# A TensorE stream that keeps the order of the program

## The chip, the cores and the metric

The kernel runs on one core of a Trainium2 chip. A core has five engines that work side by side, each on its own list of instructions and in the order of that list: TensorE (PE, matrix products), VectorE (DVE), ScalarE (ACT), GpSimd (POOL) and SyncE (SP, which here issues DMA transfers). An instruction that needs a result of another engine, or a buffer that another engine still reads, waits at the head of its list on a semaphore. The metric is the device time of one execution in microseconds (us).

## The reference

One inference step of a two-layer streaming encoder on 1024 prompt tokens and 32 sample tokens (1056 in all), width 1024, in float32. Cut to what matters:

```python
for l in range(2):
    sh1, sc1, g1, sh2, sc2, g2 = split(silu(c) @ w_ada[l] + b_ada[l], 6)     # adaLN columns
    u = x * (1 + sc1) + sh1
    if l == 0:      # mLSTM: q, k, v, gates, o from u @ w_in; a short convolution and silu on q and k
        y = mlstm_mixer(u, ...)          # 4 heads; state C (256 x 128), n, m carried from chunk to chunk
    else:           # shared k, v = (x * (1 + kv_scale) + kv_shift) @ w_kv
        q = u @ w_q
        y = softmax(q k^T / 8 + bias over own chunk and 8 previous ones) v @ w_out
    x = layer_norm(ALPHA * x + (1 + g1) * y)
    u = x * (1 + sc2) + sh2
    f = square(relu(u @ w_up[l])) @ w_down[l]
    x = layer_norm(ALPHA * x + (1 + g2) * f)
```

Inside a head the mLSTM needs per chunk the scores of the chunk, the values `num`, a new state, and a norm of the head's output. Outputs are `x`, the states, and the newest keys and values.

## The kernel before

**Products.** Tokens stand along the free dimension, features on the partitions, in three blocks of 384, 384 and 288 tokens (`TBS`). A float32 product is three passes over two float32r parts of each operand (`proj`, L111 to L120), so a 128-column tile of a product over 1024 features is 24 matmuls. Weights come by DMA as raw float32 and are split into their two parts by ACT and by DVE or POOL (`split`, L87 to L90).

**Stages, in order.**
- Start: the first adaLN columns come from TensorE (`ada`, L392); the tokens are transposed on TensorE (`xps`, L375) and modulated by ACT and DVE into U; `v_proj` (L440 to L475) makes the values and gate inputs of head 0, tile by tile (`v_0_0` to `v_0_8`, L455 to L457).
- Gates: `gate_rows` (from L477) transposes the gate inputs (`gt`, L492), runs the recurrences of the gates on DVE and ACT up to `stk` (L520), yields, and then transposes the result back on TensorE (`ae_ps`, L527).
- mLSTM: for each head, `qk_proj` and `v_proj` of the next head are advanced tile by tile, and after each tile the generator `mlstm` (L587 to L690) of the current head does one step: `scores` of chunk i (L616, L617), `values` of chunk i-1 (`num` L634 to L636, the state's `cu` L638, then a chain of small DVE and ACT operations up to `hn`, L664), and `heads` of chunk i-2 (`hT`, L672). `num` and `cu` share two PSUM banks (`nmt`). At the same time the adaLN columns of the rest of layer 0 are multiplied on DVE (`ada_l0`, through `ada_cols`, L223 to L253: products L236, transpose L243, sum `cx` L244) and every eight columns go once through TensorE (`adas`, L250).
- `o_proj` for the output gates, in two halves; then `flow.finish()`, which drains all side work; then the output projection (`op_a`), layer norm (means and variances by TensorE, `mean_n` and `var_n`, L843) and the MLP of layer 0 (`up`, `dn`).
- Layer 1: query projection (`q`), cached keys and new keys and values (`put_keys`, transposes `kt_c` L1138; `kv` products), banded attention (scores `s` L1225, softmax on DVE, ACT and POOL, transposes `pt` L1255, values `pv` L1275), output projection, MLP, and the last layer norm.

**What sets the order.** Side work is written as generators. A `Flow` (L47 to L72) holds them; `flow.tick(us)` after each tile of main work subtracts us from each generator's wait and advances those whose wait is over, and `flow.finish()` runs them out. So the program text has one order, in which main tiles and side steps alternate. Before, this order isn't the order on the engines: a list scheduler of the framework goes over the whole program with its own estimates of durations and puts each engine's instructions in the order in which it expects them to be ready. It works on each engine; the PSUM banks and SBUF buffers follow from it.

Of the kernel before, what the change touches and what calls it, by code (L numbers as in the profile page):

```python
# [8 lines left out]
F32 = mybir.dt.float32  # L9
# [6 lines left out]
P = 128  # L16
D = 1024
KC = D // P                     # feature chunks
TP = 1024                       # prompt tokens
TS = 32                         # sample tokens  # L20
T = TP + TS
NT = T // P + 1                 # token tiles, the last one holds the sample
# [4 lines left out]
NH = 4                          # mLSTM heads  # L27
CH = 128                        # mLSTM chunk
NCK = TP // CH
SAMPLE_C = NCK                  # index of the sample's mLSTM chunk  # L30
# [3 lines left out]
def segs(t0, n):  # L34
    """Pieces (offset, length, conditioning column) of a token block."""
    out = []
    if t0 < TP:
        m = min(t0 + n, TP) - t0
        out.append((0, m, 0))
        if m < n:  # L40
            out.append((m, n - m, 1))
    else:
        out.append((0, n, 1))
    return out


class Flow:  # L47
    """Side work, as generators that yield how long (us) the tensor engine should do something else first."""
# [27 lines left out]
def trunk_kernel(ctx: ExitStack, tc: tile.TileContext, a, o):  # L76
    nc = tc.nc
    flow = Flow()
# [4 lines left out]
    # ------------------------------------------------------------------ tools  # L83
# [3 lines left out]
    def split(dst_h, dst_l, src, eng=None):  # L87
        """dst_h + dst_l == src exactly, both parts in float32r."""
        nc.scalar.copy(dst_h, src)  # L89
        (eng or nc.vector).tensor_sub(dst_l, src, dst_h.bitcast(F32))  # L90

    def wtile(name, srcs, ncols=256, pool=None, eng=None, between=None):
        """A block of 4 contraction chunks x ncols columns, split. srcs: (dst slice fn, dram ap)."""
        raw = raw_tile([P, 4, ncols], f"raw_{name}")
        for dst, src in srcs(raw):
            nc.sync.dma_start(dst, src)
        if pool is None:
            w = ring.tile([P, 2, 4, ncols], F32R, tag="wc", name=f"w_{name}", bufs=6)
        else:
            w = pool.tile([P, 2, 4, ncols], F32R, tag="h", name=f"w_{name}", bufs=5)  # L100
        if between:
            between()
        split(w[:, 0], w[:, 1], raw, eng)
        return w

    def wblock(name, src, r0, c0, eng=None):
        """rows r0..r0+511, columns c0..c0+255 of src."""
        return wtile(name, lambda raw: [(raw, src[r0:r0 + 512, c0:c0 + 256].rearrange("(k p) c -> p k c", p=P))],
                     eng=eng)

    def proj(ps, n, halves, j, mov):  # L111
        """ps[:, :n] = the 128 columns j of the weight halves times mov(hl, k), three f32r passes."""
        nk = 4 * len(halves)
        for k in range(nk):
            w = halves[k // 4]
            wh = w[:, 0, k % 4, j * P:(j + 1) * P]
            wl = w[:, 1, k % 4, j * P:(j + 1) * P]
            nc.tensor.matmul(ps, wh, mov(0, k), start=(k == 0), stop=False)  # L118
            nc.tensor.matmul(ps, wh, mov(1, k), start=False, stop=False)  # L119
            nc.tensor.matmul(ps, wl, mov(0, k), start=False, stop=(k == nk - 1))  # L120

    # one activation table set serves every function used below
    nc.scalar.preload_act_table_set("natural_log_exp_and_others")

    # -------------------------------------------------------------- constants
    ident = cp.tile([P, P], F32, name="ident")
    make_identity(nc, ident)
    sel = cp.tile([P, 32], F32, name="sel")             # sel[32 a + j, j] = 1
# [8 lines left out]
    # x0T / x1T: the residual stream, transposed, while the mixers need its room  # L137
# [6 lines left out]
    # ------------------------------------------------- per-feature parameters  # L144
# [10 lines left out]
    comb = cp.tile([P, 3, KC, 2, 2], F32, name="comb")   # fused norm scale / shift per (norm, chunk, cond)  # L155
# [29 lines left out]
    def bank(name):  # L185
        """All eight banks in turn, for the phases that need no classes of them."""
        bank_n[0] += 1
        return (tpt, nmt, adat, mmt, tpt, nmt, mmt, mmt)[bank_n[0] % 8](name)
# [17 lines left out]
    # silu(c) = c * exp(min(c, 0) - ln(1 + exp(-|c|)))  # L206
# [16 lines left out]
    def ada_cols(src, c0, base, nch, mk, tmp_f, step, raw_f=raw_tile):  # L223
        """ada[:, base..base+nch-1] = silu(c) @ src[:, c0..c0+128*nch-1] + bias, multiplied on the vector engine."""
# [34 lines left out]
    def ada_fix(base, parts):  # L259
        """1 + scale and (1 + gate) / alpha, in place."""  # L260
        for i, kind in parts:
            ap = ada[:, base + i * KC:base + (i + 1) * KC, :]
            if kind == "sc":
                nc.vector.tensor_scalar_add(ap, ap, 1.0)
            else:
                nc.vector.tensor_scalar(ap, ap, 1.0, 1.0 / ALPHA, op0=ALU.add, op1=ALU.mult)

    def combine(ni, g, b, sc, sh):
        """(xn * g + b) * sc + sh as xn * G + B."""
# [27 lines left out]
    def bias_table():  # L297
        # relative-position bias, reversed and padded: e_d[h, x] = 8 * table[h, clip(575 - x) + 128]
# [9 lines left out]
        # bias_d[h, i, j] = 8 * (bias of query i against band key j)  # L308
        nc.sync.dma_start(bias_d, bass.AP(e_d.tensor, e_d.offset + 63, [[640, 16], [-1, 64], [1, 576]]))

    # --------------------------------------------------- u of layer 0, U tile
# [10 lines left out]
    def modulate(src, n, scale, shift, dst_h, dst_l, tmp, eng=None):  # L322
        """dst_h + dst_l = src * scale + shift (per-partition columns)."""
# [11 lines left out]
    YL = TP + 6 + TS            # conv stream: 3 history columns in front of each sequence  # L335
# [50 lines left out]
    def ada_start(half):  # L386
        """Shift and 1 + scale of the first mixer, for one half of the features."""
# [28 lines left out]
    # ------------------------------------------------------------ mLSTM mixer  # L416
# [4 lines left out]
    def neglogsig(dst, src):  # L421
        """dst = ln(sigmoid(src)) = min(src, 0) - ln(1 + exp(-|src|))."""
# [55 lines left out]
    def gate_rows():  # L478
# [17 lines left out]
        neglogsig(tt, fr)                                   # lf  # L496
# [7 lines left out]
        nc.vector.tensor_sub(stk[0:NH], ig, br)             # a = ig - b  # L504
        nc.vector.tensor_sub(rr, br, mr)                    # r = b - m
# [65 lines left out]
    def o_proj(hs, after):  # L571
        """G (holding the normed heads) *= mhn_g * sigmoid(o)."""
# [14 lines left out]
    def mlstm(h, qT, kT, vts):  # L587
# [3 lines left out]
        # decay logits above the diagonal count as -inf  # L591
# [36 lines left out]
        def values(c):  # L628
# [16 lines left out]
            # normaliser and head norm: h = num / dn, (h - mean) * rsqrt(var + eps)  # L645
# [60 lines left out]
    def first_half(part):  # L706
        """The first token block's products with the first half of the features, while the rest of ada loads."""
# [85 lines left out]
    # ------------------------------------------------- shared by both layers  # L793
# [6 lines left out]
    def open_acc(l, order):  # L800
        """The residual, one tile per token block; the blocks are released in `order`."""
# [18 lines left out]
    def make_layer(acc, pp, uo):  # L820
        """Post-norm and MLP on a transposed residual; uo(hl, k, t0, n) is where u is kept."""
# [3 lines left out]
        def norm(ti, ni, nm, w, after=None):  # L825
            """acc <- layer norm; u <- its modulation for the next products."""
# [6 lines left out]
            def halves(s, name):  # L833
                """s[:, 0] as two parts in float32r."""
                sr = tmp_t([P, 2, n], f"{name}r_{nm}", F32R)
                split(sr[:, 0], sr[:, 1], s[:, 0])
                return sr

            def total(sr, name):
                """The mean over the features, on every partition."""  # L840
# [50 lines left out]
        def pieces(t0, n):  # L891
            """A range of tokens in the residual's tiles: (offset, length, columns)."""
# [7 lines left out]
        def norm_out(tiles, put, y_tile_, gb, final):  # L900
            """Layer norm to token layout, without a modulation: put(token, tokens, result tile)."""
# [48 lines left out]
        def add_gated_at(t0, n, ps, gate, fc):  # L950
            """The same for any range of tokens."""
# [86 lines left out]
    # --------------------------------------------------------- layer 0, rest  # L1038
# [43 lines left out]
    # ------------------------------------------------- layer 1: q, shared k/v  # L1082
    # qo(c)[:, e, gp, r*64 + i]: queries of chunk c of head r in group 2*gp + e, both float32r parts
    # stacked along the partitions; later [:, part, gp, r*64 + i] holds the outputs' parts.
    # One tile and pool per token block (blocks start at every sixth chunk).
    qo_cm, QOT = [], []

    def qo(c):
        return QOT[c // 6][:, :, :, c % 6, :]
# [39 lines left out]
    def put_keys(src, m, pos, nm):  # L1129
        """src [m tokens, 256]: keys of the 4 groups, to both parts of kk at key position pos."""  # L1130
# [66 lines left out]
    # ------------------------------------------------------- banded attention  # L1197
# [21 lines left out]
    def softmax_unit(qst, g, k0, nk, bt, off, nm):  # L1219
        """p [128 rows, off + nk] = softmax (from the negated scores) over the keys k0..k0+nk-1; `off` zero columns in front."""  # L1220
# [23 lines left out]
    def transposed(ps_, wid, e, nm):  # L1244
        """The probability tiles of one group, keys on the partitions: [128 keys, tile, rows]."""
# [37 lines left out]
    def att_group(gp, c, e):  # L1283
        """Scores now, transposes some steps later, values (after the second group) another step later."""
# [34 lines left out]
    # --------------------------------------------- layer 1: out, norm and MLP  # L1319
# [96 lines left out]
```

## Time and profile before

| | |
|---|---|
| median of 3 runs | 2562.2 us (2561.2 to 2562.53) |
| span of the profiled execution | 2562.6 us |
| TensorE busy | 2493.5 us, 97% |
| DVE, ACT, POOL busy | 1686.0, 895.3, 339.5 us |
| DMA | 201.20 MB, 79 GB/s over the span |

The stages in the profiled execution, as I place them by the products they begin with: start to 90 us, mLSTM and gates to 438, output projection and norm to 560, MLP of layer 0 to 1224, its last norm and the query projection to 1400, keys and values to 1466, attention to 1677, output projection and norm to 1856, last MLP to 2490, last norm to the end.

How to read it: a row of a timeline has the start, the duration, the engine, the line in the kernel, the operation with its output and inputs, the shapes and a count; in brackets stands the idle time before it and what ended it. PEld is TensorE's loading of weights. A row of waits has the engine, the instruction that waited, what it waited for, and the total, the number and the longest of these waits. A row of windows has a stretch of time, its length, then for each engine busy time and count, the granted TensorE clock (1.00 is full), the DMA engines' share and GB/s.

### The profile page before, as it was taken

The numbers are of one execution on the slowest core, as the hardware profiler recorded it, in microseconds if no ns is written. First come the engines' busy times: TensorE is split into PE (matmuls) and PEld (weight loads), VectorE is DVE, ScalarE is ACT, GpSimd is POOL, SyncE is SP. The second block draws the span as 40 slices with busy tenths as digits, with TensorE's granted clock in tenths as the row PEclk, the third lists the DMA queues.
The fourth block names the chain that finished last, engine by engine and source line by source line (L and its number), as shares of the span: only waits on it lengthen the run. The fifth ranks groups of instructions, "written<-read, shape, count | busy, mean of one in ns | idle before, by whom it ended". The sixth has DMA issues, their size and how long they took to land.

```text
span 2562.6 us, 40022 instructions
## 1 busy us (share of the span) xinstructions
PE 2493.5 (97%) x15784; PEld 2371.5 (93%) x15784; DVE 1686.0 (66%) x3825; ACT 895.3 (35%) x1903; POOL 339.5 (13%) x455
## 2 busy tenths in 40 slices
PE   7999999999999999999989999999999999999998
PEld 3899899999999999999989876789999999999997
DVE  3899999778679678766696676637644334343437
ACT  3654456242212211221256566625411211221212
POOL 0111100251000000000053143405300000000003
PEclk9999999999999999999999999999999999999999
DMA  7532323412224224223113400051111111111101
GB/s 235 161 91 88 93 82 110 142 34 84 89 91 131 92 86 137 83 91 120 58 68 116 97 4 1 1 159 34 50 50 42 42 50 42 49 51 41 44 31 68
DMA packets 192064, 201.20 MB, mean 79 GB/s; under 512 B 9337, under 2 KB 180749, under 8 KB 191877
## 3 DMA queue, kind: packets, MB, share of 16 engines
q1 hardware_dynamic: 191876, 198.65, 25.4%
q8 instruction: 124, 2.03, 0.3%
q14 instruction: 64, 0.52, 0.1%
HBM read 183.38 MB, written 17.60 MB: 78 GB/s over the span
## 4 chain that ended last, share of the span: by engine, by line
PE 82%; DVE 7%; DMA 2%; ACT 2%; issue 1%; POOL 1%; SPq 0%; ACTq 0%; DVEq 0%; POOLq 0%
PE dn L118 10%; PE up L118 9%; PE dn L120 9%; PE up L119 9%; PE up L120 9%; PE dn L119 9%; PE pv L1275 3%; PE s L1225 2%; PE pt L1255 2%; DVE ada_room L236 1%; DMA ada_room<-in_w_ada_dram 1%; PE o L118 1%; PE o L120 1%; PE o L119 1%; PE q L118 1%
## 5 line engine op out<-in xcount | busy, mean ns | idle before, releaser
L118 PE MATMUL dn<-h,w_dn 128*128 128x384 f32 (+2 forms) x1568 | 505.9, 323 | 0.0
L120 PE MATMUL dn<-h,w_dn 128*128 128x384 f32 (+2 forms) x1568 | 501.9, 320 | 0.0
L119 PE MATMUL dn<-h,w_dn 128*128 128x384 f32 (+2 forms) x1568 | 497.8, 318 | 0.0
L955 DVE SCALAR_TENSOR_TENSOR acc<-dn,ada,acc 128x384 f32<-128x384 f32 (+5 forms) x536 | 243.7, 475 | 235.8 <-PE dn L120 234.1
L118 PEld LDWEIGHTS dn<-h,w_dn 128*128 128x128 f32 x1568 | 294.5, 188 | 0.8 <-PE yt L914 0.2
L119 PEld LDWEIGHTS dn<-h,w_dn 128*128 128x128 f32 x1568 | 294.2, 188 | 0.1
L120 PEld LDWEIGHTS dn<-h,w_dn 128*128 128x128 f32 x1568 | 294.0, 188 | 0.0
L995 DVE TENSOR_TENSOR r<-r 128x384 f32<-128x384 f32 (+1 forms) x192 | 104.2, 544 | 282.7 <-ACT h L994 282.1
L993 ACT ACTIVATE r<-up 128x384 f32<-128x384 f32 (+1 forms) x192 | 88.9, 463 | 470.6 <-PE up L120 456.2
L118 PE MATMUL up<-U,w_up 128*128 128x384 f32 (+1 forms) x768 | 250.2, 326 | 0.0
L119 PE MATMUL up<-U,w_up 128*128 128x384 f32 (+1 forms) x768 | 249.1, 324 | 0.0
L120 PE MATMUL up<-U,w_up 128*128 128x384 f32 (+1 forms) x768 | 248.7, 324 | 0.0
L118 PE MATMUL up<-u,w_up 128*128 128x384 f32 (+1 forms) x768 | 248.5, 324 | 0.0
L119 PE MATMUL up<-u,w_up 128*128 128x384 f32 (+1 forms) x768 | 248.4, 323 | 0.0
L120 PE MATMUL up<-u,w_up 128*128 128x384 f32 (+1 forms) x768 | 248.3, 323 | 0.0
L89 ACT CAST w_up<-raw_up 128x1024 fp32r<-128x1024 f32 x64 | 66.9, 1049 | 411.1 <-PE dn L120 274.3
L236 DVE SCALAR_TENSOR_TENSOR aacc<-rada,cs,aacc 128x256 f32<-128x256 f32 x448 | 190.4, 478 | 0.0
L118 PEld LDWEIGHTS up<-U,w_up 128*128 128x128 f32 x768 | 145.1, 189 | 0.1
L120 PEld LDWEIGHTS up<-U,w_up 128*128 128x128 f32 x768 | 145.1, 189 | 0.0
L119 PEld LDWEIGHTS up<-U,w_up 128*128 128x128 f32 x768 | 145.1, 189 | 0.0
L120 PEld LDWEIGHTS up<-u,w_up 128*128 128x128 f32 x768 | 144.3, 188 | 0.0
L119 PEld LDWEIGHTS up<-u,w_up 128*128 128x128 f32 x768 | 144.2, 188 | 0.0
(317 smaller groups left out, 5403.0 us busy)
## 6 DMA issues: line engine op xcount, KB each, us to landing
raw_up<-in_w_up_dram SPq DMA_DIRECT2D x64, 512.0 KB
raw_dn<-in_w_down_dram SPq DMA_DIRECT2D x64, 512.0 KB
rada<-in_w_ada_dram SPq DMA_DIRECT2D x48, 512.0 KB
ada_room<-in_w_ada_dram SPq DMA_DIRECT2D x32, 512.0 KB
rada<-in_w_ada_dram SPq DMA_DIRECT2D x32, 256.0 KB
rada<-in_w_ada_kv_dram SPq DMA_DIRECT2D x16, 512.0 KB
acc<-xsp SPq DMA_DIRECT2D x4, 1536.0 KB
rc<-rc_d SPq DMA_DIRECT2D x8, 528.0 KB
```

What stands on the lines that cost most here:

```text
L89: nc.scalar.copy(dst_h, src)
L118: nc.tensor.matmul(ps, wh, mov(0, k), start=(k == 0), stop=False)
L119: nc.tensor.matmul(ps, wh, mov(1, k), start=False, stop=False)
L120: nc.tensor.matmul(ps, wl, mov(0, k), start=False, stop=(k == nk - 1))
L236: nc.vector.scalar_tensor_tensor(acc[:, cnd], raw[:, k], sc, acc[:, cnd], op0=ALU.mult, op1=ALU.add)
L955: nc.vector.scalar_tensor_tensor(xs, ps[:, off + o:off + o + mm_], gate[:, fc, cnd:cnd + 1], xs, op0=ALU.mult, op1=ALU.add)
L993: nc.scalar.activation(r, ps[:, :n], AF.Relu)
L995: nc.vector.tensor_mul(r, r, r)
L1225: nc.tensor.matmul(s[:, b, :w], qst, kk[i][:, g, k0 + j0:k0 + j0 + w], start=(i == 0), stop=(i == 1))
L1255: nc.tensor.transpose(pt[:kp, j - j0, pr * P:(pr + 1) * P], ps_[pr][:, j * P:j * P + kp], ident)
L1275: nc.tensor.matmul(pv[64 * e:64 * e + 64, :nq], V[:kp, vt0 + j, g * 64:(g + 1) * 64], pts[e][:kp, j, :nq], start=(j == 0), stop=(j == nt - 1))
```

## The change

One line is added to the kernel. Inside that context, the scheduler takes TensorE's instructions in the order in which the program issues them; the other engines' instructions are still ordered by the scheduler, which now sees a fixed TensorE order.

```diff
 @with_exitstack
 def trunk_kernel(ctx: ExitStack, tc: tile.TileContext, a, o):
     nc = tc.nc
+    ctx.enter_context(tc.manual_schedule(engines={mybir.EngineType.PE}))
     flow = Flow()
```

Nothing else of what the kernel does is touched (comments were removed, so that each later line of the changed kernel has a number one higher). No product, transfer or buffer is added or taken away.

## The prediction

> **What bounds the kernel now.** I read the page first: its busy shares (name, busy us, share, instructions) and the first line of its chain.
> ```profile
> span 2562.6 us, 40022 instructions
> PE 2493.5 (97%) x15784; PEld 2371.5 (93%) x15784; DVE 1686.0 (66%) x3825; ACT 895.3 (35%) x1903; POOL 339.5 (13%) x455
> PE 82%; DVE 7%; DMA 2%; ACT 2%; issue 1%; POOL 1%; SPq 0%; ACTq 0%; DVEq 0%; POOLq 0%
> ```
> TensorE (PE) is busy for 97% of the span and is the bound; 69 us in 2562.6 is all it ever stands still. So the change has little to win, and what it can lose is every microsecond in which PE waits with nothing else in front of it. Next the busy time by stretch: mixer of layer 0, its MLP, attention, the last MLP.
> ```profile
> core 0: us, PE busy (x) PEld busy (x) DVE busy (x) ACT busy (x) POOL busy (x), PEclk, DMA share, GB/s
> 100.00:435.00 335.00, 328.34 (x2143) 309.88 (x2142) 306.93 (x887) 174.44 (x467) 42.50 (x109) 0.99 0.30 90
> 640.00:1224.00 584.00, 584.00 (x3668) 582.20 (x3667) 427.27 (x937) 121.65 (x200) 0.00 (x0) 1.00 0.33 101
> 1466.00:1677.00 211.00, 206.84 (x1403) 148.14 (x1402) 139.43 (x505) 134.64 (x375) 85.21 (x164) 0.97 0.08 18
> 1856.00:2490.00 634.00, 634.00 (x3930) 633.81 (x3929) 250.41 (x435) 131.89 (x216) 0.00 (x0) 1.00 0.15 45
> ```
> The MLPs have no idle time at all. In the mixer VectorE (DVE) is busy 306.93 of 335 us: there PE stays full only because it always has a product ready that needs nothing from DVE. Last, PE's own waits (what, for whom: us in total, times, longest).
> ```profile
> PE var_n L843 <- ACT qr_n L89: 6.3, 2, 4.5
> PE tp_c L203 <- DMA c_rows<-in_c_sample_dram: 5.6, 1, 5.6
> ...
> PE q L118 <- DVE acc L955: 4.0, 2, 3.3
> ...
> PE cu L638 <- DVE hn L664: 3.9, 6, 2.2
> ...
> PE xps L375 <- ACT xt L380: 2.9, 2, 2.4
> ```
> No wait is above 6.3 us in total. Thirty-six recurrent steps wait 3.9 us together at `cu`: that shows how well the scheduler's order hides that chain.
>
> **The change, part by part.** No instruction is added or removed; of PE's 15,290 matched instructions 2,492 change place, by up to 196 places, and 1,264 of DVE's, 446 of ScalarE's (ACT), 57 of POOL's and 83 of SP's follow (SP's by at most 11, so transfers keep their order). Inside the two MLPs PE's order is the same, so they cost 0. I price each place where an instruction that waits now stands in front of work that used to cover its wait.
>
> *Start.* Rows of a timeline are start, duration, engine, line, operation.
> ```profile
> 73.05 0.28 PE L455 MATMUL v<-w_v,U 128*128 128x264 f32 x1
> 73.17 0.29 PE L456 MATMUL v<-w_v,U 128*128 128x264 f32 x1
> 73.30 0.56 PE L375 MATMUL xps<-ident,xr 128*128 128x128 f32 x3
> ...
> 83.50 0.56 PE L375 MATMUL xps<-ident,xr 128*128 128x128 f32 x3
> ...
> 87.40 0.51 PE L492 MATMUL gt<-ident,g 128*36 128x128 f32 x3
> ```
> The last six `xps` groups of the third block start at 73.30 to 83.50, paced by ACT and DVE that empty them, and `v` matmuls every 0.12 us fill the pauses. Program order finishes these transposes before `v_0_6`, `v_0_7`, `v_0_8`. Each of those is 24 matmuls, 2.9 us: 8.7 us that ran mostly beside the pacing now run after it; 83.50 to 87.40 shows 3.9 of it already behind, so +4.8. The second block's transposes stand likewise ahead of `v_0_3` (+2), and the `gt` transposes ahead of the first `qk` (+1). Sum **+8**, bounds 5 and 10 (all 8.7 plus 1).
>
> *Gate transposes.*
> ```profile
> 88.99 0.20 PE L492 MATMUL gt<-ident,g 32*36 32x32 f32 x1
> ...
> 107.03 1.08 ACT L520 ACTIVATE stk<-tt 4x1056 f32<-4x1056 f32 x1 [0.37 <-DVE tt L519]
> ...
> 108.16 0.72 PE L527 MATMUL ae_ps<-ident,stk 36*128 36x36 f32 x9 [2.42 <-ACT stk L520]
> ```
> From the last `gt` (89.19) to `stk` (108.11) the chain takes 18.9 us. Program order has only the three `qk_0` tiles before it (24 matmuls each; at 34.99/196 = 0.18 us, from a row below, and three quarters of that for 288 columns, 11.6 to 11.8 us), so it stands ahead of nine matmuls of the next tile that precede it now. Stall 7.3 against 2.42: **+5** (3 to 7). Earlier placing of the first scores and values wins about 2 back: **-2** (0 to -4).
>
> *The mLSTM steps of heads 0 to 3.*
> ```profile
> 135.25 0.60 PE L634 MATMUL num<-vt,sT 128*128 128x257 f32 x2
> ...
> 146.57 0.54 DVE L664 TENSOR_SCALAR hn<-num,sm 128x256 f32<-128x256 f32 x1
> ...
> 147.25 0.67 PE L638 MATMUL cu<-vt,kw 128*128 128x257 f32 x2
> ...
> 187.70 0.53 DVE L664 TENSOR_SCALAR hn<-num,sm 32x256 f32<-32x256 f32 x1
> ```
> `cu` of chunk 1 (147.25) starts as `hn` of chunk 0 ends: it takes the bank that `hn` frees, 11.3 us after `num`. Those 11 us PE spent on later projections. In program order a step is scores, `num`, `cu`, `hT`, then one projection tile: 2.9 us (`v`) or 4.2 us (`qk`), with 1.65 us of its own matmuls, and `cu` blocks what follows. For each chunk I added up the DVE work that the new order puts between its first statistics and its `hn`, 1.6 us for the two ACT steps in it, and took off the tiles that stand between: the excess is 12, 11.6, 7 and 8.7 us for the four heads, 39 in all. The nine `hn` of head 0 come 41.1/8 = 5.1 us apart now, about a step's length, so if DVE drains its backlog in PE's stalls little is lost: lower bound 10. Upper 45. I take **+32**, nearer the sum, as the chain of one chunk is serial and two banks leave no slack.
>
> *The last adaLN columns before the output projection.*
> ```profile
> 438.32 0.26 PE L250 MATMUL adas<-cx,sel 128*32 128x16 f32 x8
> 438.51 0.44 PE L118 MATMUL op_a<-U,w_oa 128*128 128x384 f32 x1
> ...
> 473.83 0.69 DVE L244 TENSOR_REDUCE cx<-ada_room 128x16 f32<-128x512 f32 x1
> ...
> 475.16 0.26 PE L250 MATMUL adas<-cx,sel 128*32 128x16 f32 x8
> ```
> Two calls of the same side work: after the first `adas`, `op_a` starts at once; the second needs DVE's reduction that ends at 474.52. What runs between, on PE (columns: busy, count, clock) and on DVE:
> ```profile
> 438.50:475.00 36.50, 34.99 (x196) 1.00 0.71 230
> ...
> 438.50:475.00 36.50, 29.04 (x66) 1.00 0.71 230
> ```
> 196 `op_a` matmuls, 34.99 us, fill the wait. In program order both `adas` stand before the first `op_a`, since the side work is drained ahead of the projection. This cover goes whole, and the work behind it isn't shortened: its transfers keep their place on SP. **+34**. DVE's 29.04 us contain the additions that `op_a` feeds; I put these and what may come later at 7 at most, so 22 is the lower bound, and 38 (36.5 and a slow restart) the upper. It is the largest single term. It is not hidden by PE's being late before: DVE's adaLN work stands, in the new DVE order too, behind the last gate of the o projection, which waits for PE.
>
> *The MLP's entry* at 1224.8 waits for a weight half: **+1**.
>
> *Query projection* (the two windows show PE busy, count, clock).
> ```profile
> 1314.48 0.55 DVE L329 TENSOR_TENSOR U<-ut_n,U 128x384 fp32r<-128x384 f32 x1
> ...
> 1298.00:1308.50 10.50, 6.53 (x36) 0.99 0.22 71
> 1308.50:1316.70 8.20, 8.20 (x40) 0.81 0.11 39
> ```
> `q_0` needs pieces of U up to the one at 1314.48. Before, matmuls of `q_1`, `q_2` and `q_3` ran in those 18.7 us; now `q_0` stands first and they wait behind it. About 56 of the 76 matmuls in these windows are of that kind, 0.18 us each: **+10** (7 to 13).
>
> *Keys.*
> ```profile
> 1405.91 0.44 PE L1138 MATMUL kt_c<-ident,kd_c 128*128 128x128 f32 x2 [1.01 <-ACT kd_c L1132]
> ...
> 1409.33 0.44 PE L1138 MATMUL kt_c<-ident,kd_c 128*128 128x128 f32 x2 [0.59 <-DVE kd_c L1133]
> ...
> 1405.90:1415.60 9.70, 6.82 (x51) 1.00 0.26 70
> ```
> The third and fourth cached key tiles stand directly before `kv0_0` and `kv1_0`; 6.82 us of `kv` ran in their waits: **+6** (4 to 8).
>
> *Attention.*
> ```profile
> 1521.81 0.65 PE L1275 MATMUL pv<-pT,V 128*64 128x256 f32 x2
> 1522.39 0.80 PE L1225 MATMUL s<-k,QO 128*128 128x288 f32 x4
> ```
> The pair of `pv` matmuls that ran alone moves behind the scores and joins its group; it took 0.58 us to the next start. At most 0.3 us a chunk in some 20 chunks is won, and 2 to 4 lost in the first chunks, which have little between score and value: **-2** (-8 to +6).
>
> *Clock.* After the 3.3 us wait for `q` the granted clock fell to 0.81 over 8.2 us: 1.6 us lost. Two new long stalls (`adas`, `ae_ps`): **+3** (0 to 6).
>
> **Sum:** 8 + 5 - 2 + 32 + 34 + 1 + 10 + 6 - 2 + 3 = +95 us on the profiled span of 2562.6, which stands 0.4 us above the median of the runs, 2562.2 (2561.2 to 2562.53): 2657 us, +3.7%.
>
> **Rivals.**
> *Half of it is taken up.* DVE drains in each stall, so later stalls shrink: mixer +15, adaLN +27, start and gates +10, `q` and keys +14, rest +2: +68, 2630 us. For it: DVE's steps are near the PE step's length. Against: DVE is 92% busy there and its order is fixed.
>
> *The clock falls at every step.* If half of the 36 steps stall past 3 us, each costs the 1.6 us shown at `q`: 18 x 1.6 = 29 more, 2686 us. Against: 3 us is more than most of the excesses above. The Trainium skill, in "TensorE: Matmul & The Clock Gate", section "HAM oscillation — how this bites in real kernels", speaks for this rival: it tells of a kernel whose waits of 3 to 5 us between short bursts throttled the clock again and again. By that rule the stalls hurt twice; the row at 1308.50 agrees for one stall, and no row of before shows a train of them.
>
> *Faster.* Unbroken tiles run closer: 34 `pv` pairs at 0.58 us, all won, would give up to 20 us, over 0.2% if less than 15 us of waits appear elsewhere. Against: the `adas` wait alone has a floor of 22.
>
> *The order stays.* 2,492 moved PE instructions rule it out; if those orders cost nothing, no change.
>
> **How the numbers follow.** Forecast (2643 to 2672) 0.5; taken up (2612 to 2643) 0.22; clock (2672 to 2700) 0.2; faster 0.04; no change 0.02; beyond 0.02. A measurement of this kernel tells about 0.2%, 5 us. The range takes the forecast and most of its two neighbours: 2620 to 2695. Faster 0.04, within 0.2% 0.02, slower 0.94.
>
> **What would show it.** In the changed profile: a PE wait for DVE's `cx` at `adas` of 25 us or more with an empty slice near 500 us; waits at `cu` for `hn` grown from 3.9 to some 30 us; `q_0` as one wait near 10 us; `kt_c` waits of 9 or more; both MLPs as long as before. Wrong if `adas` waits for little (DVE ran ahead), if `cu` stays under 10 us, or if the lone pairs of `pv` prove dearer than the waits.

## The result and the profile after

The changed kernel takes 2691.88 us (median of 4 runs, 2688.05 to 2696.48) against 2562.36 us for the kernel before, measured beside it: ratio 1.0511, 95% interval 1.0497 to 1.0525. It is 5.1% slower. The profiled execution has a span of 2694.7 us, 132.1 us more than before; it is the slowest of the four, so the differences by place below come out some 3 us larger than the difference of the medians, 129.5.

The page of the changed kernel, the same three lines:

```profile
span 2694.7 us, 40023 instructions
PE 2504.8 (93%) x15784; PEld 2395.9 (89%) x15784; DVE 1694.9 (63%) x3825; ACT 898.2 (33%) x1903; POOL 336.2 (12%) x455
...
PE 78%; DVE 11%; ACT 2%; DMA 2%; issue 2%; POOL 1%; DVEq 0%; ACTq 0%; SPq 0%; POOLq 0%
```

TensorE is busy for 11 us more than before and idle for 190 us instead of 69. In the chain of work that ended last, DVE's share rises from 7% to 11%. Busy time by stretch (start, head 0 of the mLSTM, the stretch before the output projection, MLP of layer 0, last MLP):

```profile
core 0: us, PE busy (x) PEld busy (x) DVE busy (x) ACT busy (x) POOL busy (x), PEclk, DMA share, GB/s
54.50:104.20 49.70, 36.71 (x228) 32.39 (x227) 30.39 (x77) 28.59 (x57) 1.29 (x6) 0.81 0.66 199
...
153.50:219.00 65.50, 50.81 (x316) 45.61 (x314) 58.81 (x187) 27.30 (x81) 6.76 (x28) 0.87 0.27 83
...
524.50:560.00 35.50, 0.65 (x18) 0.53 (x18) 25.94 (x60) 9.20 (x15) 2.31 (x1) 0.55 0.69 229
...
661.00:1342.00 681.00, 677.76 (x4247) 675.47 (x4246) 506.94 (x1107) 158.75 (x275) 28.06 (x28) 1.00 0.31 95
...
1985.00:2625.00 640.00, 639.21 (x3965) 638.81 (x3964) 252.61 (x439) 131.92 (x216) 0.00 (x0) 1.00 0.14 44
```

The MLPs are as full as before. The loss lies in the stretches with side work, where the granted clock is below 1 as well, and in one empty stretch of 35 us. TensorE's waits (in total, times, longest):

```profile
PE adas L251 <- DVE cx L245: 35.1, 2, 34.9
PE cu L639 <- DVE hn L665: 26.0, 16, 7.5
PE cu L639 <- DVE sm L662: 14.5, 2, 7.8
PE xps L376 <- ACT xt L381: 13.6, 11, 3.5
PE q L119 <- ACT U L325: 11.0, 2, 9.9
PE cu L639 <- DVE sm L661: 7.9, 1, 7.9
...
PE kt_c L1139 <- ACT kd_c L1133: 4.4, 1, 4.4
...
PE kt_c L1139 <- DVE kd_c L1134: 4.1, 2, 3.1
...
PE cu L639 <- DVE sm L653: 3.2, 1, 3.2
```

The four rows of `cu` add up to 51.6 us, against 3.9 before (`hn` and the `sm` rows are links of the same chain, which frees the bank). Every wait that the forecast named is here; the rows of `kt_c` make 8.5 us, a little under the 9 that it asked for.

To see where the 132.1 us came in, I took the starts and ends of the same tiles in both traces; the difference between them is how late the changed kernel is at that place:

| stretch, up to | late by there, us | this stretch | forecast |
|---|---|---|---|
| start, end of `qk_0` | 17.7 | +17.7 | +8 |
| gate transposes, end of `qk_4` | 20.8 | +3.1 | +5 |
| first scores and values | 20.4 | -0.4 | -2 |
| mLSTM heads 0 to 3, start of `o_4_0` | 86.1 | +65.7 | +32 |
| second `adas` and output projection | 121.3 | +35.2 | +34 |
| norm, first `up` of layer 0, to the first `dn` | 119.0 | -2.3 | 0 |
| MLP's end | 120.3 | +1.3 | +1 |
| query projection, first `kt` | 131.9 | +11.6 | +10 |
| keys and values | 142.2 | +10.3 | +6 |
| attention, first output product | 130.2 | -11.9 | -2 |
| output projection, last MLP, end | 132.1 | +1.9 | 0 |

The clock's +3 of the forecast is inside these stretches. The heads missed by 34 us, the start by 10, the attention by 10 the other way. The experiments ask for the causes of the attention and of the heads first.

### The profile page after: what moved, and what is told of

Same layout as the page of the kernel before. It is cut to its first block, busy times and chain, and to the rows that moved or that the text cites. A ratio compares the mean times of both kernels' runs of the same rounds, so it can differ in the third digit from the quotient of the medians.

```text
span 2694.7 us, 40023 instructions
## 1 busy us (share of the span) xinstructions
PE 2504.8 (93%) x15784; PEld 2395.9 (89%) x15784; DVE 1694.9 (63%) x3825; ACT 898.2 (33%) x1903; POOL 336.2 (12%) x455
## 4 chain that ended last, share of the span: by engine, by line
PE 78%; DVE 11%; ACT 2%; DMA 2%; issue 2%; POOL 1%; DVEq 0%; ACTq 0%; SPq 0%; POOLq 0%
PE dn L119 9%; PE up L119 9%; PE dn L121 9%; PE up L121 9%; PE up L120 9%; PE dn L120 9%; PE pv L1276 2%; PE s L1226 2%; PE pt L1256 2%; DVE ada_room L237 2%; DMA ada_room<-in_w_ada_dram 1%; PE q L120 1%; PE q L121 1%; PE q L119 1%; PE op_a L119 1%
## 5 line engine op out<-in xcount | busy, mean ns | idle before, releaser
L121 PEld LDWEIGHTS up<-U,w_up 128*128 128x128 f32 x768 | 144.2, 188 | 1.0 <-DVE w_up L91 1.0
L121 PEld LDWEIGHTS up<-u,w_up 128*128 128x128 f32 x768 | 145.0, 189 | 0.0
L119 PEld LDWEIGHTS up<-u,w_up 128*128 128x128 f32 x768 | 144.9, 189 | 0.0
L120 PEld LDWEIGHTS up<-u,w_up 128*128 128x128 f32 x768 | 144.8, 189 | 0.0
L119 PEld LDWEIGHTS up<-U,w_up 128*128 128x128 f32 x768 | 144.1, 188 | 0.2
```

## The experiments

**The attention alone in program order.** One of the stretches got shorter, so it is worth having by itself. Edit to the kernel before:

```diff
+    with tc.manual_schedule(engines={mybir.EngineType.PE}):
         for gp in range(2):
             for c in range(17):
                 for e in range(2):
                     flow.add(att_group(gp, c, e))
                     flow.tick()
         flow.finish()
```

> The kernel before, with TensorE kept in program order in the attention loop alone. Theory (split value products): in the scheduler's order the first value matmul of a chunk runs alone ahead of the next scores, and each such switch of TensorE costs time; program order keeps the ten matmuls of a chunk together. In the changed kernel a chunk takes 6.94 us where it took 7.53, and the attention 12 us less. So 2550 us (2548 to 2553), faster than before by 0.4 to 0.5%. Rival (slack): attention was shorter in the changed kernel because the other engines had gained a lead in the longer phases ahead of it; then the region alone brings 4 us or less, 2558 to 2562.

Measured: 2547.77 us (5 runs) against 2560.79, ratio 0.9948, interval 0.9935 to 0.9962. It is 13 us faster than the kernel before, the whole of what the attention gained in the changed kernel.

**The same with the first value matmul back in its place.**

```diff
+                if (j, e) == (0, 1):
+                    yield
                 nc.tensor.matmul(pv[64 * e:64 * e + 64, :nq], ...)
...
-        yield
+        if not e:
+            yield
         if e:
...
-            weighted_values(gp, ...)
+            yield from weighted_values(gp, ...)
```

> As the attention-only kernel, but the first value matmul of a chunk is issued one step earlier, right behind the chunk's last transposes, which from the eighth chunk on is the order that the scheduler had chosen. Theory (split value products): the gain is gone, 2562 us (2559 to 2565), and a lone value matmul again costs about 0.58 us to the next start. Rival: the gain comes from the first chunks or from the scores; then this kernel stays at 2550.

Measured: 2560.81 us against 2560.79, ratio 1.0001, interval 0.9992 to 1.0010. One matmul per chunk carries the whole gain. A chunk in the timeline, from the scores of the second group to those of the next chunk, first in the kernel with whole value products (start, duration, operation, count of records; one matmul leaves two):

```profile
1516.08 1.29 PE L1225 MATMUL s<-k,QO 128*128 128x288 f32 x8
1517.21 1.25 PE L1255 MATMUL pt<-ident,p 128*128 128x128 f32 x10
1518.24 1.48 PE L1225 MATMUL s<-k,QO 128*128 128x288 f32 x8
1519.66 2.38 PE L1275 MATMUL pv<-pT,V 128*64 128x256 f32 x20
1521.97 1.31 PE L1255 MATMUL pt<-ident,p 128*128 128x128 f32 x10
1523.03 1.31 PE L1225 MATMUL s<-k,QO 128*128 128x288 f32 x8
```

and with the first one alone:

```profile
1517.45 1.31 PE L1225 MATMUL s<-k,QO 128*128 128x288 f32 x8
1518.60 1.25 PE L1255 MATMUL pt<-ident,p 128*128 128x128 f32 x10
1519.78 0.65 PE L1277 MATMUL pv<-pT,V 128*64 128x256 f32 x2
1520.35 1.33 PE L1225 MATMUL s<-k,QO 128*128 128x288 f32 x8
1521.61 2.37 PE L1277 MATMUL pv<-pT,V 128*64 128x256 f32 x18
1523.91 1.31 PE L1255 MATMUL pt<-ident,p 128*128 128x128 f32 x10
1524.98 1.31 PE L1225 MATMUL s<-k,QO 128*128 128x288 f32 x8
```

6.95 us against 7.53. Nine matmuls behind the scores take about as long to the next start (2.30 us) as ten do (2.31), and the lone one takes 0.57 of its own.

The traces show why. Each value matmul writes 64 of the 128 output columns, and the two heads of a group write different halves. In the first of the two kernels the 20 records of a chunk start in twos, 0.007 us apart, and the twos about 0.216 us apart: a matmul of one head and a matmul of the other run at the same time. With the first one alone, its two records start singly, and of the 18 behind the scores the last two do as well: the nine have lost a partner, and nine take ten's time. Over the whole attention the kernel before has 112 more such single records than the changed kernel (144 against 32). That makes 56 places in the row more, which at 0.216 us are 12.1 us: an estimate from the traces, beside the 11.9 that the attention gained. The groups of value matmuls (busy us, then mean ns of one), before and after, say the same: one takes as long, more of them overlap.

```profile
L1275 PE MATMUL pv<-pT,V 128*64 128x256 f32 (+3 forms) x500 | 82.6, 390 | 0.0
```

```profile
L1276 PE MATMUL pv<-pT,V 128*64 128x256 f32 (+3 forms) x499 | 64.4, 388 | 1.8 <-DVE pT L1266 1.8
```

**The last adaLN sum later.** Edit to the changed kernel: the generator of the adaLN columns stops ahead of its last `adas`, and is run out behind the first eight tiles of the output projection.

```diff
         for w in ada_cols(a["w_ada"][0], 2048, 16, 32, adat, tmp_f, ADA_C, raw_f):
+            if w == "last":
+                ada_fix(0, [(2, "g"), (4, "sc")])
+                yield 1e9
...
-        ada_fix(0, [(2, "g"), (4, "sc"), (5, "g")])
+        ada_fix(0, [(5, "g")])
...
     def end_out0(ti):
+        for _ in ada_g:
+            pass
```

> The changed kernel, with the last sum of adaLN columns (the second adas) drained behind the first eight output-projection tiles instead of ahead of them; all else in program order. Theory (lost cover): the wait of 34.9 us at adas goes to under 3, and the time falls by 30 to 35 us, from 2692 to 2657 to 2662. Rival (a DVE chain that only shows itself there): the additions of the output projection and the first norm then queue behind the adaLN work on DVE, and only 15 to 25 us come back, 2667 to 2677.

Measured: 2660.08 us, 31.8 less than the changed kernel; the wait at `adas` is gone from its list of waits. The term was cover that had been lost, and little slipped into its place: `op_a` now waits 2.8 us for its weights. In the changed kernel the stall looks like this:

```profile
524.44 0.26 PE L251 MATMUL adas<-cx,sel 128*32 128x16 f32 x8
559.55 0.31 PE L251 MATMUL adas<-cx,sel 128*32 128x16 f32 x8 [34.85 <-DVE cx L245]
559.80 0.69 PE L119 MATMUL op_a<-U,w_oa 128*128 128x384 f32 x1
```

**What holds TensorE in the heads.** My forecast gave the bank that `hn` frees as the reason for the waits at `cu`. A look at the program order shows a second one: `hT` of the chunk before stands right behind `cu` and reads the same `hn`. First, a third bank only (`adas` gives up its own bank and shares the three):

```diff
     def adat(name):
-        return pa.tile([P, 512], F32, tag="ada", name=name, bufs=1)
+        return pa.tile([P, 512], F32, tag="nm", name=name, bufs=3)
...
     def nmt(name):
-        return pa.tile([P, 512], F32, tag="nm", name=name, bufs=2)
+        return pa.tile([P, 512], F32, tag="nm", name=name, bufs=3)
```

> The changed kernel with a third bank for num and cu (adas shares it, no other class loses one). My prediction's reason was the bank: then the 51.6 us of waits at cu go to under 10 and the time falls by 40 us or more, to 2650 or less. Theory now (order): the transposes hT of the chunk before stand directly behind cu in program order and need the same hn, so the wait only moves from cu to hT: cu waits under 5 us, hT waits over 40, time 2684 to 2700.

Measured: 2682.79 us (2 runs), 9 us less than the changed kernel, 1 us below the theory's band and 33 above the 2650 that the bank alone would give. The four runs of the changed kernel lie 8.4 us apart, so the waits tell more here than the time:

```profile
PE hT L673 <- DVE hn L665: 38.6, 15, 7.8
...
PE hT L673 <- DVE sm L661: 7.1, 1, 7.1
```

`cu` no longer waits for `hn` at all, and `hT` waits 45.7 us for it instead of 51.6 at `cu`. Then `hT` one step later, with the two banks of the changed kernel:

```diff
-        for i in range(NT + 2):
+        for i in range(NT + 3):
...
-            if i >= 2:
-                heads(i - 2)
+            if i >= 3:
+                heads(i - 3)
```

(and three buffers for `hn`).

> The same later hT, with the two banks of the changed kernel. Theory (two holds, either is enough): cu still takes the bank that hn frees, so the waits stay at cu, 45 us or more, 2684 to 2697. Rival (the place of hT alone holds PE): the waits fall under 20 us, 2650 to 2660.

Measured: 2688.45 us, as the theory has it; `cu` still waits 52.4 us, in four rows. Both edits together:

> The changed kernel with three banks for num and cu, and hT of a chunk one step later in the program (scores of i, values of i-1, heads of i-3; three buffers for hn). Theory (distance): a step is 4.5 to 6 us and hn comes 4 to 17 us after num, so a second step of distance covers nearly all: waits at cu and hT together under 10 us instead of 51.6, the clock in the mixer back near full, time down by 45 to 60 us, 2632 to 2647. Rival (DVE is the bound of the mixer): the waits stay above 25 us and the time above 2660.

Measured: 2635.53 us, 56 us less than the changed kernel. The remaining waits on the chain, and head 0's window (busy of PE, PEld, DVE, ACT, POOL, then the clock):

```profile
PE cu L639 <- DVE hn L665: 5.8, 3, 3.1
...
PE cu L639 <- DVE sm L657: 2.3, 1, 2.3
PE cu L639 <- DVE sm L662: 2.2, 2, 1.4
```

```profile
153.50:219.00 65.50, 62.40 (x437) 58.54 (x436) 58.62 (x193) 31.56 (x92) 7.02 (x29) 1.00 0.32 96
```

With 0.3 in one more row, `cu` waits 10.6 us, just above the 10 expected, and `hT` doesn't wait. From the first `num` to `o_4_0` this kernel falls behind the kernel before by 14 us, the changed kernel by 68. So each hold alone keeps the loss, and DVE, busy 58.6 and 58.8 of 65.5 us in the two windows, isn't the bound that the rival made it. The clock in the window is back at 1.00 from 0.87. The whole stretch of the heads, from chunk 1's `num` to `o_4_0`, in the kernel before, the changed kernel and this one:

```profile
138.55:391.50 252.95, 248.78 (x1666) 231.31 (x1664) 230.96 (x743) 124.50 (x357) 28.48 (x92) 0.99 0.31 91
```

```profile
158.98:477.62 318.64, 265.71 (x1665) 244.85 (x1664) 244.29 (x757) 126.00 (x351) 26.52 (x92) 0.90 0.26 78
```

```profile
157.76:422.65 264.89, 251.06 (x1666) 234.00 (x1664) 230.53 (x740) 121.50 (x351) 24.03 (x92) 0.97 0.29 89
```

TensorE's idle time goes from 4.2 to 52.9 us and back to 13.8. The same matmuls are busy for 248.8, 265.7 and 251.1 us, at granted clocks of 0.99, 0.90 and 0.97: most of the slower clock came with the waits and went with them.

**Which work of DVE stands in the chain.** Two of the four taps of the short convolution are left out, so q and k are not those of the reference.

```diff
-            for i in range(1, 4):
+            for i in range(3, 4):
                 nc.vector.scalar_tensor_tensor(y[:, :N], qkp[:, i:i + N], ...)
```

> The changed kernel with two of the four taps of the short convolution on q and k left out (two of the three multiply-adds of 1.31 us on DVE for each of the eight feature blocks). Theory (the convolution stands between num and hn on DVE): the seven waits at cu of 2.5 to 7.9 us, 41.7 in sum, lie where 6 to 8 us of convolution run before hn; each shrinks by up to 2.6 us, the waits at cu fall from 51.6 to 32 to 38, and the time by 15 to 22 us, 2670 to 2677. Rival (the adaLN side work sets them): less than 6 us of the waits go, 2686 to 2692.

Measured: 2671.40 us, 20.5 less than the changed kernel, and the waits at `cu` now:

```profile
PE cu L639 <- DVE hn L665: 23.9, 16, 5.3
...
PE cu L639 <- DVE sm L654: 5.4, 2, 3.4
...
PE cu L639 <- DVE sm L653: 3.2, 1, 3.2
PE cu L639 <- DVE sm L657: 2.9, 1, 2.9
```

35.4 us in sum, 16.2 less than 51.6, for 21 us (16 x 1.31) of DVE work taken out, 13 of them (10 x 1.31) behind the first `num`. So the convolution is in the chain. One of the long waits of the changed kernel, with what DVE did ahead of it:

```profile
174.85 0.42 DVE L649 BATCH_NORM_STATS2 st<-num 128x6 f32<-128x256 f32 x1
175.19 1.30 DVE L560 SCALAR_TENSOR_TENSOR y<-qkp,pt,y 128x1059 f32<-128x1059 f32 x1
...
178.60 0.96 DVE L427 SCALAR_TENSOR_TENSOR sl<-y,sl 128x353 f32<-128x353 f32 x2
...
180.14 0.95 DVE L566 SCALAR_TENSOR_TENSOR y<-y,sl 128x353 f32<-128x353 f32 x2
```

```profile
184.18 1.20 PE L639 MATMUL cu<-vt,kw 128*128 128x257 f32 x2 [7.81 <-DVE sm L662]
```

The convolution and silu of the next head's q or k, taken in pieces between the small steps of the norm, put `hn` late, and `cu` stands 7.81 us at the head of TensorE's list. Pieces of the adaLN work stand among them too, 2.5 us between these statistics and the `hn`; what they add to the waits was not tried by itself.

**The start left to the scheduler.** The ordered region begins only behind the first v projection:

```diff
-    ctx.enter_context(tc.manual_schedule(engines={mybir.EngineType.PE}))
...
     vts = [v_proj(0, after_v0, first_half)]
     flow.finish()
+    ctx.enter_context(tc.manual_schedule(engines={mybir.EngineType.PE}))
     gates = flow.add(gate_rows(), now=True)
```

> The changed kernel, with the ordered region beginning after the first v projection, so that the scheduler orders TensorE at the start as before. Theory (the start costs its 17.7 us by itself): time falls by 14 to 18 us, 2674 to 2678. Rival (the gate chain behind it takes part back, since qk_0 then comes earlier and ae_ps waits longer): 6 to 10 us fall away, 2682 to 2686.

Measured: 2677.04 us, 14.8 less than the changed kernel, in the theory's band. The gate wait takes only a little of it back:

```profile
PE ae_ps L527 <- ACT stk L520: 5.1, 1, 5.1
```

against 4.1 in the changed kernel. Part of why the start cost more than forecast shows in these rows of the changed kernel:

```profile
89.92 0.93 PE L376 MATMUL xps<-ident,xr 128*128 128x128 f32 x3 [1.71 <-ACT xt L381]
...
91.39 0.42 PE L458 MATMUL v<-w_v,U 128*128 128x264 f32 x1
91.61 0.42 PE L456 MATMUL v<-w_v,U 128*128 128x264 f32 x1
```

The `v` matmuls that now come behind the row of waiting transposes start 0.22 us apart instead of 0.12.

## Why the prediction was right, point by point

The direction, the place of each loss and the range held: 2692 lies in 2620 to 2695, 3 us from its upper end, while the forecast itself, 2657, is 35 us too low. The time falls among those of the rival of the clock (2672 to 2700, chance 0.2) and not among the forecast's own (2643 to 2672). That the range held is in part luck: start, heads, keys and attention each lie outside their own bounds, the attention on the other side.

- *What bounds the kernel.* Right: TensorE had 69 us of idle time, and every added wait in front of ready work went onto the time nearly in full. Undoing three of them one at a time brought 31.8, 56 and 14.8 us.
- *The last adaLN columns, +34.* Right, measured +35.2 on the trace and 31.8 by the experiment.
- *MLP's entry, query projection, gate transposes, first scores.* Right within 2 us each; the wait at `ae_ps` itself is 4.1 us, where 7.3 was forecast. *Keys:* +10.3 against +6 (upper bound 8). The `kt` waits (8.5 us, against 3.3 before) account for 5.2 and a new wait of `kv` for its split weights for 2.2. The rest, 2.8, is longer busy time at a granted clock of 0.93 against 1.00; it wasn't tried.
- *The heads, +32.* The mechanism was right and the size wrong, in two ways. My own sum was 39, and I discounted it to 32 because DVE might drain in the stalls; measured at `cu` are 51.6, 47.7 more than before. The step that failed is this discount, and the working ahead of it, which counted DVE's work only from a chunk's first statistics on: in the one long wait shown above DVE comes late to those too (174.85, for a `num` whose last matmul started at 171.03). And the reason I gave, the bank, is half of it: with three banks the wait moves to `hT`, and only bank and place together free TensorE.
- *The clock, +3.* Too low. Of the 65.7 us of the heads, added idle time of TensorE is 48.8, which leaves 16.9 of longer busy time; of the 17.7 us of the start, added idle time is 14.7, which leaves 3.0. In both stretches the granted clock is lower than before, 0.90 against 0.99 and 0.85 against 0.94, and matmuls start further apart. Gate transposes, query projection and keys have 7.5 us more of the same kind, some 27 in all. So the rival *the clock falls at every step* was partly true: 2686 was its time, but it supposed 18 stalls past 3 us, and the heads have seven, of 3.2 to 7.9 us. That the 27 us are the clock's is worked out, not tried by itself; it fits that in the heads of the kernel with both holds removed, where the idle time fell by 39.1 us, the busy time fell by 14.7 as well. The Trainium skill's "TensorE: Matmul & The Clock Gate", in "HAM oscillation — how this bites in real kernels", tells of a kernel whose waits of 3 to 5 us between short bursts throttled the clock again and again. The heads agree with that; in the start a clock of 0.81 came with waits of 3.5 us at most.
- *Start, +8.* Mis-sized: +17.7. The waits at `xps` are 13.6 us instead of 2.9, and the forecast had nothing for two others: `ada` waits 5.9 us for its weights instead of 1.6, since the first `xps` and `v` matmuls no longer stand between its products, and `gt` waits 1.8. The `v` matmuls' own waits of 2.4 went, and 3.0 are the longer busy time above.
- *Attention, -2.* Mis-sized: -11.9. The step that failed is "at most 0.3 us a chunk": the two traces have 0.58 us, and the gain holds over nearly all full chunks. I had read the two records of one matmul as a pair of matmuls, and had counted on its 0.58 us less what it takes in a row. The rows before show no such price, for the nine left behind take as long as ten: the matmuls of the two heads run side by side, and taking one away leaves another without its partner.
- *Half of it is taken up* fell: outside the attention, the one stretch that gave back more than half a microsecond gave 2.3 us. *Faster* fell for the whole kernel, but its mechanism is real and is worth 13 us where it stands alone.

## What to carry to other kernels

Before pinning an engine's order, list for each instruction that waits what stood in front of it that was ready; if the program text puts it ahead of that work, its wait is the price, and it adds to the time in full when the engine is the bound. A recurrent chain that is interleaved by hand needs its distance counted in every hold, the buffer and the next reader, since freeing one alone leaves the wait: it moved to the next reader, or stayed at the buffer. An order can be good in one stage and bad in the others: here the scheduler's order is worth 142 us up to the keys and loses 12 in the attention, so the order is best fixed stage by stage.

## What the runs showed that I had not expected

- Two value matmuls of 64 output columns each, on different halves, run at the same time when they stand next to each other: their records start 0.007 us apart. One matmul taken out of its row costs 0.57 us to the next start and the row of nine saves nothing (2.30 us against 2.31 for ten); such single matmuls, one in a chunk, are worth 13 us of 2561.
- Waits of at most 3.5 us, eleven of them among the transposes, came with a granted clock of 0.81 over 50 us; matmuls of 264 columns then start 0.22 us apart instead of 0.12. With the start left to the scheduler the waits at `xps` are 2.9 us in two and the clock up to the end of the first `qk_0` tile is 0.93, against 0.85.
